# Six start addresses for the blocks of split weights, and three raw buffers for four, in a one-layer decoder kernel

## The chip, the cores and the metric

The kernel runs on one core of a Trainium2 chip. The metric is device time in microseconds (us), lower is better. A core has four engines that compute, each with its own in-order list of instructions: PE (matrix products, with a second record PEld for the loading of a product's stationary operand), DVE (elementwise arithmetic), ACT (elementwise functions and copies) and POOL. SP issues most of the transfers (DMA). All of them meet through semaphores only. SBUF is the memory on the core, 128 partitions wide; an address below is a byte offset within a partition.

## The reference

One decoder layer on 512 tokens of width 1024, with all weights in float32:

```python
h = h + 0.5 * swiglu(rms_norm(h, ffn1_norm), ffn1_w_gu, ffn1_w_down)      # width 2816
n = rms_norm(h, mix_norm)
p = n @ w_in + b_in                    # 6 x 1024 columns
a_val, a_gate, b_u, b_v, g_a, g_b = jnp.split(p, split_at, axis=-1)
y_a = conformer_conv_branch(a_val, a_gate, ...)   # GLU, causal depthwise conv of 31 taps, layer norm, swish, @ w_a_out
y_b = spatial_gating_branch(b_u, b_v, ...)        # gelu, layer norm, 128 x 128 mixing, @ w_b_out
h = h + (sigmoid(g_a) * y_a + sigmoid(g_b) * y_b) @ w_out
h = h + memory_cross_attention(rms_norm(h, xattn_norm), rms_norm(mem, mem_norm), w_q, w_kv, w_o)  # 4 heads, 256 memory tokens
h = h + 0.5 * swiglu(rms_norm(h, ffn2_norm), ffn2_w_gu, ffn2_w_down)
return rms_norm(h, final_norm)
```

## The kernel before

Activations lie channel-major: 8 tiles of 128 channels by 512 tokens, in `xhi`/`xlo` or in 50 slots of the pool `big`. Every float32 operand of a large product is split into two float32r parts, hi (a copy rounded to float32r) and lo (the rest), and `mm3` makes one product out of three matmuls: hi by hi (L106), hi weight by lo activation (L107), lo weight by hi activation (L108). In most stages the weight is the stationary operand, 128 by 128, and the activation moves with 512 columns. In `linear_rows` (L174 to L176) it is the other way round and the weight moves. The keys (`key`, tiles `pk`, 64 products) and the last output tile (`dl`, 44 products) have 256 columns.

Weights come in blocks of up to 128 by 1024 (512 KB). A block goes through three steps. `wfetch` takes a tile `raw` and issues its transfer on SP (L90). `wsplit` copies it on ACT to `hi` (L98, the CAST rows) and subtracts on DVE to get `lo` (L99). PE then reads `hi` and `lo`, 24 matmuls for a full block. There are four raw buffers, three for hi and three for lo, so a transfer waits until the DVE split of an earlier block has freed a raw buffer, and a CAST waits until PE is done with an earlier block. The memory tokens (`mem`, two blocks of 512 KB) come through the same raw buffers and are read straight from there by ACT and DVE (L185, L186, L190, L193). A raw buffer is freed by its last reader.

The order on each engine is set by a scheduler that estimates times from the program; code order is its input. A name such as `d3w8h` is the hi part of the block of `w_dn` for output tile 3 that begins at k = 8; `d3w` in a transfer's row is its raw buffer. The stages in order of time: `g`/`u` (first up projection), `d` (down projection, with the two `mem` blocks), `pk` (keys), `av`/`ag` (conv inputs), `r` (token-major rows), `gb`, `yb`, `ga`, `pv`, `ya`, `o`, attention (`pq`, `sc`, `po`, `wo`), `g`/`u` and `d` again. The depthwise convolution runs on DVE beside the matmuls (L346): tap `back` adds into a tile from element `back` on, so its output and one input begin 4 x `back` bytes into a slot and have 512 - `back` elements.

Of the kernel before, what the change touches and what calls it, by code (L numbers as in the profile page):

```python
# [10 lines left out]
F32 = mybir.dt.float32  # L11
F32R = mybir.dt.float32r
# [4 lines left out]
P = 128  # L17
# [26 lines left out]
NV = _o  # L44
VW = 416


@with_exitstack
def conformer_layer(ctx: ExitStack, tc: tile.TileContext, xT, memT, vecs, rows, w_gu1, w_dn1, w_in_f, w_in_t,
# [5 lines left out]
    wpool = ctx.enter_context(tc.tile_pool(name="wpool", bufs=1))  # L55
# [7 lines left out]
    h = const.tile([P, DT, T], F32, name="h")  # L63
# [19 lines left out]

    def wfetch(srcs, name):

        raw = wpool.tile([P, 1024], F32, tag="raw", name=name, bufs=4)
        n = 0
        for src in srcs:
            m = src.shape[1] * src.shape[2]
            nc.sync.dma_start(out=raw[:, n:n + m], in_=src.rearrange("p k c -> p (k c)"))  # L90
            n += m
        return raw[:, :n]

    def wsplit(raw, c, name):
        n = raw.shape[1]
        hi = wpool.tile([P, 1024], F32R, tag="whi", name=name + "h", bufs=3)[:, :n]
        lo = wpool.tile([P, 1024], F32R, tag="wlo", name=name + "l", bufs=3)[:, :n]
        S.copy(out=hi, in_=raw)  # L98
        V.tensor_tensor(out=lo, in0=raw, in1=hi.bitcast(F32), op=ALU.subtract)  # L99
        return hi.rearrange("p (k c) -> p k c", c=c), lo.rearrange("p (k c) -> p k c", c=c)  # L100

    def wload(src, name):
        return wsplit(wfetch([src], name), src.shape[2], name)
# [49 lines left out]
    def linear_pair(wsrcs, ahi, alo, name):  # L153

        accs = [new_ps(f"{name}{i}") for i in range(2)]
        for k0 in range(0, DT, DT // 2):
            ks = slice(k0, k0 + DT // 2)
            whi, wlo = wsplit(wfetch([w[:, ks, :] for w in wsrcs], f"{name}w{k0}"), P, f"{name}w{k0}")
            for k in range(k0, k0 + DT // 2):
                for i in range(2):  # L160
                    c = i * DT // 2 + k - k0
                    mm3(accs[i], whi[:, c, :], wlo[:, c, :], ahi[k], alo[k], k == 0, k == DT - 1)
        return accs
# [73 lines left out]
    def pair(name):  # L237
        return slot(name + "h", F32R), slot(name + "l", F32R)
# [29 lines left out]
    for k in range(DT):  # L268
        nc.sync.dma_start(out=h[:, k, :], in_=xT[:, k, :])
        if k == 0:  # L270
            nc.sync.dma_start(out=vec[:, :NV], in_=vecs)
        if k % 2 == 0:
            j, k0 = k // 2 % 2, k // HF * HF
            raws.append(wfetch([w_gu1[j][:, k0:k0 + HF, :], w_gu1[FT + j][:, k0:k0 + HF, :]], f"first{k}"))
    firsts = [(new_ps(f"fg{j}"), new_ps(f"fu{j}")) for j in range(2)]
    ws = []
    for k in range(DT):
        split_x(k, "ffn1_norm")
        if k % HF < 2:
            ws.append(wsplit(raws[len(ws)], P, f"first{k}"))  # L280
        if k % HF == 0:
            continue
        for kk in (k - 1, k) if k % HF == 1 else (k,):
            for j in range(2):
                whi, wlo = ws[kk // HF * 2 + j]
                for i in range(2):
                    c = i * HF + kk % HF
                    mm3(firsts[j][i], whi[:, c, :], wlo[:, c, :], xh[kk], xl[kk], kk == 0, kk == DT - 1)
# [227 lines left out]
    for i in range(DT):  # L516
# [6 lines left out]
        hi, lo = pair(f"aa{i}")  # L523
# [7 lines left out]
    for m in range(DT):  # L531
# [4 lines left out]
        hi, lo = pair(f"mg{m}")  # L536
# [13 lines left out]
    oh, ol = [], []  # L550
# [3 lines left out]
    for i in range(DT // 2):  # L554
        hi, lo = pair(f"k{i}")
# [111 lines left out]
    for i in range(2):  # L667
        ts = slice(i * T // 2, (i + 1) * T // 2)
        pd = new_ps(f"dl{i}")[:, :T // 2]
        for k in range(FT):  # L670
            whi, wlo = ws[k // 8]
# [71 lines left out]
```

## Time and profile before

| what | us |
|---|---|
| median of 2 runs | 1323.42 (1323.26 to 1323.59) |
| the profiled execution, whole | 1324.05 |
| its span, first to last instruction | 1322.3 |
| around the span | 1.75 |
| PE busy | 1299.4 (98%) |

The profiled execution is 0.63 us over the median, so a difference worked out on its rows is put on the median unchanged. Rows of PE overlap, since a matmul is pipelined: the time that one costs is the distance between two starts, and its own length says little. The rows of PEld lie under those of PE.

### The profile page before, as it was taken

Reading aid. Unit: us, or ns where it says so; the run is one execution under the profiler, and the core shown is the slowest. Engines: PE = TensorE matmul, PEld = TensorE weight load, DVE = VectorE, ACT = ScalarE, POOL = GpSimd, SP = SyncE. Lnnn points to the kernel's source line nnn. Section 1 sums busy time; section 2 is a strip of 40 time slices with the busy share of each in tenths; the row PEclk is TensorE's granted clock in tenths of the full one; section 3 lists DMA queues with packets and bytes.
Section 4 is the critical chain, followed back from the end, with each engine's and each line's share of the span. In section 5 each row is a group of like instructions: output and inputs, shape, how many; then the busy total and the mean of one; then the engine's idle time right before and its main releaser. Section 6 shows DMA issues by size and latency. Waiting matters only on the chain.

```text
span 1322.3 us, 14923 instructions
## 1 busy us (share of the span) xinstructions
PE 1299.4 (98%) x5968; PEld 1079.5 (82%) x5968; DVE 776.7 (59%) x1078; ACT 456.3 (35%) x618; POOL 19.4 (1%) x31
## 2 busy tenths in 40 slices
PE   7999999999999999999999999999999999999996
PEld 6888888888898888888788788887888888888886
DVE  5544444434367999999996776554644444442323
ACT  5323333223233223343224744333433332322221
POOL 0000000000020000100000000000000000000000
PEclk9999999999999999999999999999999999999998
DMA  6333323333353333332233333102332232333221
GB/s 212 108 98 98 96 96 96 88 101 114 112 183 114 102 96 96 104 98 78 93 98 113 110 112 110 66 20 72 127 101 96 96 96 96 96 88 104 88 72 64
DMA packets 40661, 132.47 MB, mean 100 GB/s; under 512 B 4433, under 2 KB 7249, under 8 KB 40593
## 3 DMA queue, kind: packets, MB, share of 16 engines
q1 hardware_dynamic: 39872, 129.17, 31.1%
q0 software_dynamic: 720, 2.36, 0.6%
q8 instruction: 46, 0.75, 0.2%
q14 instruction: 23, 0.18, 0.0%
HBM read 129.42 MB, written 2.10 MB: 99 GB/s over the span
## 4 chain that ended last, share of the span: by engine, by line
PE 97%; DVE 1%; ACT 1%; DMA 0%; issue 0%; SPq 0%; DVEq 0%; POOLq 0%; ACTq 0%
PE g L106 6%; PE u L107 6%; PE g L107 6%; PE u L106 6%; PE u L108 6%; PE g L108 6%; PE d L106 6%; PE d L108 6%; PE d L107 6%; PE r L175 2%; PE r L176 2%; PE r L174 2%; PE ya L106 1%; PE ya L107 1%; PE gb L108 1%; PE ga L106 1%
## 5 line engine op out<-in xcount | busy, mean ns | idle before, releaser
L346 DVE SCALAR_TENSOR_TENSOR cv<-ap,vec,cv 128x494 f32<-128x494 f32 (+24 forms) x240 | 163.4, 731 | 0.4
L246 DVE TENSOR_TENSOR u<-u,n4rb 128x512 f32<-128x512 f32 x22 | 15.2, 691 | 66.8 <-PE u L108 66.8
L246 DVE TENSOR_TENSOR u<-u,n1rb 128x512 f32<-128x512 f32 x20 | 13.8, 691 | 62.6 <-PE u L108 62.6
L242 DVE TENSOR_TENSOR g<-g,n4rb 128x512 f32<-128x512 f32 x22 | 15.2, 691 | 48.4 <-PE g L108 44.3
L242 DVE TENSOR_TENSOR g<-g,n1rb 128x512 f32<-128x512 f32 x20 | 13.8, 691 | 40.1 <-PE g L108 40.1
L248 DVE TENSOR_TENSOR f<-s,u 128x512 f32<-128x512 f32 x44 | 30.4, 692 | 5.4 <-ACT s L244 1.1
L244 ACT ACTIVATE s<-g 128x512 f32<-128x512 f32 x44 | 27.9, 633 | 0.1
L263 DVE SCALAR_TENSOR_TENSOR h<-d,h 128x512 f32<-128x512 f32 x15 | 10.4, 692 | 29.5 <-PE d L108 29.5
L194 DVE TENSOR_TENSOR acc<-acc,sq 128x512 f32<-128x512 f32 x34 | 23.3, 685 | 0.1
L193 ACT ACTIVATE sq<-h 128x512 f32<-128x512 f32 x34 | 21.2, 623 | 1.3 <-DVE h L263 0.2
L186 DVE SCALAR_TENSOR_TENSOR xlo<-h,vec,xhi 128x512 fp32r<-128x512 f32 x24 | 17.8, 747 | 5.0 <-ACT xhi L185 5.0
L185 ACT ACTIVATE xhi<-h,vec 128x512 fp32r<-128x512 f32 x24 | 17.2, 717 | 1.6 <-DVE h L628 1.1
L545 DVE TENSOR_TENSOR h<-o,h 128x512 f32<-128x512 f32 x8 | 5.5, 692 | 12.5 <-PE o L108 12.5
L534 DVE TENSOR_TENSOR ga<-ya,sga 128x512 f32<-128x512 f32 x8 | 5.5, 689 | 12.3 <-PE ya L108 12.3
L389 DVE TENSOR_TENSOR uv<-r,br 128x512 f32<-128x512 f32 x16 | 10.5, 687 | 0.1
L106 PE MATMUL fg<-xhi,first0h 128*128 128x512 f32 x4 | 2.2, 550 | 8.2 <-ACT first0h L98 8.2
L589 ACT ACTIVATE pr<-sc,mx 128x256 f32<-128x256 f32 x16 | 7.4, 470 | 6.4 <-DVE mx L586 6.4
L390 ACT ACTIVATE uv<-uv 128x512 f32<-128x512 f32 x16 | 9.0, 620 | 1.2 <-DVE uv L389 1.2
L569 DVE TENSOR_TENSOR qt<-pq,n3rb 128x512 f32<-128x512 f32 x8 | 5.3, 686 | 6.9 <-ACT n3rb L220 4.1
L628 DVE TENSOR_TENSOR h<-wo,h 128x512 f32<-128x512 f32 x8 | 5.4, 688 | 6.3 <-PE wo L108 6.3
L106 PEld LDWEIGHTS fg<-xhi,first0h 128*128 128x128 f32 x4 | 1.0, 251 | 8.4 <-ACT first0h L98 8.2
L585 DVE TENSOR_REDUCE mx<-sc 128x2 f32<-128x512 f32 x8 | 5.5, 692 | 3.7 <-PE sc L108 3.3
(4300 smaller groups left out, 4251.1 us busy)
## 6 DMA issues: line engine op xcount, KB each, us to landing
h<-xT SPq DMA_DIRECT2D x8, 256.0 KB, 5.8
first<-w_gu SPq DMA_DIRECT2D x8, 256.0 KB, 5.9
d0w<-w_dn SPq DMA_DIRECT2D x4, 512.0 KB, 3.5
d1w<-w_dn SPq DMA_DIRECT2D x4, 512.0 KB, 3.7
d2w<-w_dn SPq DMA_DIRECT2D x4, 512.0 KB, 3.4
d3w<-w_dn SPq DMA_DIRECT2D x4, 512.0 KB, 3.4
d4w<-w_dn SPq DMA_DIRECT2D x4, 512.0 KB, 3.6
d5w<-w_dn SPq DMA_DIRECT2D x4, 512.0 KB, 3.5
```

What stands on the lines that cost most here:

```text
L106: PE.matmul(out, whi, ahi, start=start, stop=False)
L107: PE.matmul(out, whi, alo, start=False, stop=False)
L108: PE.matmul(out, wlo, ahi, start=False, stop=stop)
L174: PE.matmul(accs[t], a_h, whi[:, k - k0, :], start=k == 0, stop=False)
L175: PE.matmul(accs[t], a_h, wlo[:, k - k0, :], start=False, stop=False)
L176: PE.matmul(accs[t], a_l, whi[:, k - k0, :], start=False, stop=k == nk - 1)
L194: V.tensor_tensor(out=acc, in0=acc, in1=sq, op=ALU.add)
L242: V.tensor_tensor(out=g1, in0=pg, in1=rb, op=ALU.mult)
L244: S.activation(s1, g1, AF.Silu)
L246: V.tensor_tensor(out=u1, in0=pu, in1=rb, op=ALU.mult)
L248: V.tensor_tensor(out=f, in0=s1, in1=u1, op=ALU.mult)
L346: V.scalar_tensor_tensor(out=o, in0=aps[i][:, :T - back], scalar=w, in1=o, op0=ALU.mult, op1=ALU.add)
```

## The change

The tiles of hi and lo grow by 64 elements, and the block lies in them at an offset that goes round with every third block: hi at element 0, 16 or 32 (byte 0, 64, 128), lo at element 4, 2 or 48 (byte 16, 8, 192). In the kernel before, all hi, lo and raw tiles begin at multiples of 256 bytes, as all slots of `big` do, and a product's 128 by 128 weights follow each other at 512 bytes. After the change hi lies at multiples of 64 bytes, one lo in three too, one lo in three 16 bytes and one in three 8 bytes past such a multiple. The raw pool has three tiles in place of four. The six larger tiles take 1.5 KB more and the missing raw tile 4 KB less, so `big` and the pools behind it move down by 2,560 bytes and stay at multiples of 256. The offsets go round in step with the three buffers, so each buffer keeps one place.

```diff
+SHIFTS = ((0, 4), (16, 2), (32, 48))
...
     def wfetch(srcs, name):
-        raw = wpool.tile([P, 1024], F32, tag="raw", name=name, bufs=4)
+        raw = wpool.tile([P, 1024], F32, tag="raw", name=name, bufs=3)
...
+    shift = [0]
+
     def wsplit(raw, c, name):
         n = raw.shape[1]
-        hi = wpool.tile([P, 1024], F32R, tag="whi", name=name + "h", bufs=3)[:, :n]
-        lo = wpool.tile([P, 1024], F32R, tag="wlo", name=name + "l", bufs=3)[:, :n]
+        oh, ol = SHIFTS[shift[0] % 3]
+        shift[0] += 1
+        hi = wpool.tile([P, 1024 + 64], F32R, tag="whi", name=name + "h", bufs=3)[:, oh:oh + n]
+        lo = wpool.tile([P, 1024 + 64], F32R, tag="wlo", name=name + "l", bufs=3)[:, ol:ol + n]
         S.copy(out=hi, in_=raw)
         V.tensor_tensor(out=lo, in0=raw, in1=hi.bitcast(F32), op=ALU.subtract)
```

The instructions are the same ones. On PE, POOL and SP they also keep their order, apart from what they wait for. On ACT and DVE the order differs at two places. The lines of the changed kernel have numbers higher by 6 (L98 there is L104). The first place is in the first down projection, where ACT reads the first memory block (m0h, m2h, macc) between the CASTs of weight blocks. Before:

```order
L98 CAST d1w16h<-d1w_1935 128x768
L190 ACTIVATE acc_1786<-h 128x512
L185 ACTIVATE m0h<-mem_2052,vec 128x256
L190 ACTIVATE macc<-mem_2052 128x256
L185 ACTIVATE m0h<-mem_2052,vec 128x256
L185 ACTIVATE m2h<-mem_2052,vec 128x256 x2
L98 CAST d2w0h<-d2w_1964 128x1024
L98 CAST d2w8h<-d2w_1994 128x1024
L98 CAST d2w16h<-d2w_2024 128x768
```

and after:

```order
L104 CAST d1w16h<-d1w_1935 128x768
L196 ACTIVATE acc_1786<-h 128x512
L104 CAST d2w0h<-d2w_1964 128x1024
L191 ACTIVATE m0h<-mem_2052,vec 128x256
L196 ACTIVATE macc<-mem_2052 128x256
L191 ACTIVATE m0h<-mem_2052,vec 128x256
L104 CAST d2w8h<-d2w_1994 128x1024
L191 ACTIVATE m2h<-mem_2052,vec 128x256 x2
L104 CAST d2w16h<-d2w_2024 128x768
```

The CASTs of d2w0 and d2w8 have moved ahead of readers of the memory block, and the splits of these two blocks on DVE likewise. The second place is on ACT at the end of the attention's output projection, where xhi and sq prepare the next norm. Before:

```order
L98 CAST wo5w0h<-wo5w_7029 128x1024
L185 ACTIVATE xhi<-h,vec 128x512
L190 ACTIVATE acc_6150<-h 128x512
L185 ACTIVATE xhi<-h,vec 128x512
L193 ACTIVATE sq<-h 128x512
L98 CAST wo6w0h<-wo6w_7066 128x1024
L185 ACTIVATE xhi<-h,vec 128x512
L193 ACTIVATE sq<-h 128x512
```

and after:

```order
L104 CAST wo5w0h<-wo5w_7029 128x1024
L191 ACTIVATE xhi<-h,vec 128x512
L196 ACTIVATE acc_6150<-h 128x512
L191 ACTIVATE xhi<-h,vec 128x512
L199 ACTIVATE sq<-h 128x512
L191 ACTIVATE xhi<-h,vec 128x512
L199 ACTIVATE sq<-h 128x512
L104 CAST wo6w0h<-wo6w_7066 128x1024
```

The CAST of wo6w0 stands one pair of xhi and sq later, and its split on DVE one xlo later.

## Rows read from the trace of the kernel before

**Rows 1.** Page, part 1: busy us, share of the span, instructions.

```profile
PE 1299.4 (98%) x5968; PEld 1079.5 (82%) x5968; DVE 776.7 (59%) x1078; ACT 456.3 (35%) x618; POOL 19.4 (1%) x31
```

**Rows 2.** Page, part 4: the chain that ended last.

```profile
PE 97%; DVE 1%; ACT 1%; DMA 0%; issue 0%; SPq 0%; DVEq 0%; POOLq 0%; ACTq 0%
```

**Rows 3.** Timeline, down projection: start us, length us, what; 42 matmuls apart.

```profile
299.87 0.39 PE L108 MATMUL d<-f4h,d3w0l 128*128 128x512 f32 x1
...
309.39 0.39 PE L108 MATMUL d<-f18h,d3w16l 128*128 128x512 f32 x1
```

**Rows 4.** Windows: busy us of the engines, granted clock (1.00), DMA share, GB/s.

```profile
290.00:300.00 10.00, 10.00 (x46) 8.29 (x45) 4.19 (x6) 3.45 (x6) 0.00 (x0) 1.00 0.40 113
```

**Rows 5.** Timeline of PE, keys with 256 columns, 16 matmuls apart.

```profile
381.90 0.28 PE L106 MATMUL pk<-m0h,pk3w0h 128*128 128x256 f32 x1
...
383.82 0.28 PE L107 MATMUL pk<-m4l,pk3w0h 128*128 128x256 f32 x1
```

**Rows 6.** Groups of PEld, down projection: busy us, mean ns of one.

```profile
L108 PEld LDWEIGHTS d<-f5h,d0w0l 128*128 128x128 f32 x1 | 0.2, 188 | 0.0
```

**Rows 7.** Groups by form of DVE, convolution taps, 380 to 640 us.

```profile
L346 DVE SCALAR_TENSOR_TENSOR cv<-ap,vec,cv 128x510 f32<-128x510 f32 x8 | 6.0, 748 | 0.0
L346 DVE SCALAR_TENSOR_TENSOR cv<-ap,vec,cv 128x508 f32<-128x508 f32 x7 | 5.2, 743 | 0.0
L346 DVE SCALAR_TENSOR_TENSOR cv<-ap,vec,cv 128x496 f32<-128x496 f32 x6 | 4.4, 727 | 0.0
```

**Rows 8.** Transfers: count, KB each, median us to landing; av2w is the longest.

```profile
d5w<-w_dn SPq DMA_DIRECT2D x4, 512.0 KB, 3.5
...
av2w<-w_in_f SPq DMA_DIRECT2D x1, 512.0 KB, 7.5
```

**Rows 9.** Timelines of SP and DVE at the start.

```profile
10.39 1.01 SPq L90 DMA_DIRECT2D first<-w_gu  x2
...
8.17 1.23 DVE L99 TENSOR_TENSOR first0l<-first,first0h 128x1024 fp32r<-128x1024 f32 x1 [2.39 <-ACT first0h L98]
```

**Rows 10.** Timelines of SP, ACT and DVE, down projection with its memory blocks.

```profile
268.65 0.33 SPq L90 DMA_DIRECT2D mem<-memT  x1
...
272.25 0.51 ACT L185 ACTIVATE m0h<-mem,vec 128x256 fp32r<-128x256 f32 x1 [3.92 <-DMA mem<-memT]
277.68 1.05 ACT L98 CAST d2w8h<-d2w 128x1024 fp32r<-128x1024 f32 x1 [2.47 <-issue]
...
281.94 0.69 DVE L263 SCALAR_TENSOR_TENSOR h<-d,h 128x512 f32<-128x512 f32 x1 [1.95 <-PE d L108]
308.68 1.23 DVE L99 TENSOR_TENSOR d4w8l<-d4w,d4w8h 128x1024 fp32r<-128x1024 f32 x1 [3.42 <-ACT d4w8h L98]
317.12 1.05 ACT L98 CAST d5w0h<-d5w 128x1024 fp32r<-128x1024 f32 x1 [3.90 <-PE d L107]
357.26 0.90 ACT L185 ACTIVATE m6h<-mem,vec 128x256 fp32r<-128x256 f32 x2
```

**Rows 11.** Transfers of yaw; timelines of DVE, ACT and PE before the product with w_a.

```profile
DMA to landing us min/median/max: 2.9/3.8/4.0
...
730.64 1.22 DVE L99 TENSOR_TENSOR pv1w4l<-pv1w,pv1w4h 128x1024 fp32r<-128x1024 f32 x1
735.39 1.06 ACT L98 CAST yaw4h<-yaw 128x1024 fp32r<-128x1024 f32 x1 [0.34 <-PE pv L176]
737.43 1.37 ACT L460 ACTIVATE vt<-pv,nmr 128x512 f32<-128x512 f32 x2 [0.46 <-PE pv L176]
738.70 0.61 ACT L181 CAST aa0h<-lny 128x512 fp32r<-128x512 f32 x1
739.36 0.73 PE L106 MATMUL ya<-aa0h,yaw0h 128*128 128x512 f32 x2 [1.28 <-ACT aa0h L181]
```

**Rows 12.** Timelines of ACT and PE, attention's output projection.

```profile
926.51 1.05 ACT L98 CAST wo6w0h<-wo6w 128x1024 fp32r<-128x1024 f32 x1
935.63 0.39 PE L106 MATMUL wo<-oo0h,wo6w0h 128*128 128x512 f32 x1
```

## Prediction

> **What bounds the kernel now.** I read the page's busy times first: PE is busy 98% of the span, every other engine at most 59%, but for the weight loads that run under PE's own matmuls [rows 1]. A busy PE is not yet PE at its peak, so the chain of work that ended last comes next: 97% of it is PE, and the transfers, SP and the other engines together hold 2% [rows 2]. So the time is a number of matmuls times the distance between two starts, plus a few places where PE waits. That distance is read off a timeline. In the down projection 42 matmuls of 512 columns take 309.39 - 299.87 = 9.52 us, 226.7 ns each [rows 3], at a granted clock of 1.00, the 2.4 GHz level [rows 4]. 512 columns at 2.4 GHz are 213.3 ns, so 13.4 ns in each matmul are not columns. A matmul of 256 columns takes 1.92 us / 16 = 120 ns [rows 5], 13.3 ns over its 106.7. The excess is thus the same for a long and a short matmul.
>
> Two things can move the time: the 226.7 ns, if PE reads the shifted blocks differently, and the places where PE waits for a block, since blocks now have three raw buffers.
>
> **The change part by part.**
>
> *Where PE reads hi and lo.* No instruction is added, so the price is a change of the distance times a count. The 5,968 matmuls [rows 1] are at most 5,968 / 3 = 1,989 that read a lo, and two lo in three leave the 64-byte multiples: 1,326 at most. All hi and the remaining lo stay at multiples of 64 bytes. No operand of PE before lies 8 or 16 bytes off such a multiple at full width, so the trace doesn't show this read, and I bound it. What is near: DVE reads and writes shifted runs all through the convolution, and a run of 510 elements that begins at byte 8 takes 748 ns, one of 508 at byte 16 743, one of 496 at byte 64 727 [rows 7]. That is 21 ns for 14 elements, which falls smoothly with the count and has no step between 8, 16 and 64 bytes. On PE a load takes 188 ns of the 226.7 ns of its matmul [rows 6], so 38.7 ns may be added before one is late. I take 0, by the rows of DVE and that cover. If the cover goes, the price is in the second rival below; the other end is the whole 13.4 ns given back, the first rival.
>
> *What DVE and ACT write.* The split on DVE now writes lo at byte 8, 16 or 192, and ACT writes hi at 0, 64 or 128. By the same rows of DVE this costs nothing. A change of 10 ns in one of some 245 splits would be 2.5 us of DVE time in all, on an engine that is 59% busy [rows 1, 7]. I put it at 0.
>
> *Three raw buffers, at the start.* Each transfer of a block waits until the DVE split of the block three places earlier (before: four) is through, and SP issues in order, so everything behind it waits too. The first wait that is new is that of the fourth block: it needs the split of first0, which ends at 8.17 + 1.23 = 9.40 us. Its transfer is issued at 10.39 anyway [rows 9], so neither it nor the last slice of h behind it on SP is later. Cost 0.
>
> *Three raw buffers, in the stages.* A full block is 24 x 0.2267 = 5.44 us of PE, so a transfer that waits for one block more comes about 5.4 us later. The least cover is in the down projection, because a memory block keeps its raw buffer long: the second has landed by about 304 us and its last part is first read at 357.26 [rows 10]. Two buffers are then left for the weights. Take d5w0: its transfer must now wait for the split of d4w8, which ends at 308.68 + 1.23 = 309.91; with 3.5 us to landing [rows 8] it is there at 313.4, and its CAST starts at 317.12, released by PE [rows 10]. 3.7 us are left. Cost 0.
>
> *The memory blocks themselves and the moved CASTs.* The first memory block loses its cover altogether: m0h starts the moment it lands, 268.65 + 3.6 = 272.25. Now the transfer waits for the split of d2w0. The CAST of d2w0, which the new order puts first, can start one block before that of d2w8, at 277.68 - 5.44 = 272.24; its split on DVE ends some 2.3 us later (1.05 + 1.23), at 274.5, and the block lands at 278.1. ACT waits there, and behind m0h, macc and m0h (at most 0.51 us each) stands the CAST of d2w8: it starts at about 279.6 in place of 277.68, and lo is done at 281.9. PE ends the tile before at 281.94 and needs d2w8 a block later, at 287.4 [rows 10]. The cover is 5.5 us, so cost 0. The second memory block makes d4w8 late by about the same 2 us; that turns the 3.7 us above into 1.7, still positive.
>
> *The product with w_a.* Here PE does wait: 1.28 us until aa0h [rows 11]. The second block of yaw could be issued when pv1w2 was split; now it waits for pv1w4, split at 730.64 + 1.22 = 731.86. Two issues of some 0.4 us apart and at most 4.0 us to landing give 736.2, where its CAST started at 735.39. So the CAST is about 0.9 us late. ACT is in order, and behind the CAST are queued vt and then aa0h, which ends PE's wait. vt itself waited 0.46 us for PE, so ACT had that much room [rows 11]. What is left is 0.9 - 0.46 = 0.4 us, and from then on PE has no other work to fill it: **+0.4 us**. It is the one place where I find the depth of the buffers on the path.
>
> *The attention's output.* The CAST of wo6w0 is moved behind one more xhi and sq and its transfer waits one block longer. It stood at 926.51, and PE first reads it at 935.63 [rows 12]. After 2.3 us of split 6.8 us of cover remain, for a move of 1 to 2 us. Cost 0.
>
> The sum is +0.4 us: 1324.05 becomes 1324.45 for the profiled execution, and on the median 1323.42 + 0.4 = **1323.8 us**.
>
> **The rivals.**
>
> *The excess is a conflict of places, and the shift removes it.* If loads and moving reads meet in the same part of SBUF because all begin at multiples of 256 bytes, six places would take them apart. At most all 5,968 matmuls lose 13.4 ns: 80 us, 1243 us. For it speaks only that the excess is there and that all places before are round. Against it: weights at six buffers and in eight steps of 512 bytes, beside moving operands at other places, all give the one distance, as 42 in a row show [rows 3]; and the excess is 13.3 ns for half the columns too [rows 5], where a conflict in streaming would halve.
>
> On this the Trainium skill, "TensorE: Matmul & The Clock Gate", section "Wait — 56ns, not 53.3ns?", has 215.7 ns from start to start for 512 columns when warm; this trace is 11 ns above it. As an estimate from that page, 5,968 x 11 ns = 66 us would be to be had, 1258 us. The same page, section "Step-by-step: what each phase is for", says that the load and the moving operand have read ports of their own, so a load takes nothing from the running matmul; by that rule the places can't matter and this rival falls. The trace agrees as far as it goes, since loads lie under matmuls that keep one distance.
>
> *A shifted lo costs its load a second pass* (the other side). If a start off the line makes PE read a column's words twice, the load is doubled at two lo in three. It decides when a load takes over 226.7 ns. The load's share of PE's time is between 120 ns, since PE loads once every 120 ns in the narrow products [rows 5], and 188 ns [rows 6]. Doubled, the first is 240: 13.3 ns over, on the wide ones; the 64 + 44 narrow products hold 72 shifted lo, at 120 ns more each. (1,326 - 72) x 13.3 + 72 x 120 = 25 us, 1349 us. Doubled, the second is 376: 1,326 x 149.3 = 198 us, 1521 us. Against it: DVE's shifted runs cost nothing [rows 7]; for it, that PE's loads are another reader and this read has no row.
>
> *Two raw buffers are too few beside a memory block.* A buffer is busy for the time to landing plus 2.3 us of split, and two of them feed PE while (landing + 2.3) / 2 is under 5.44, which is up to a landing of 8.6 us. The median is 3.5 and the longest for a weight block in one view 7.5 [rows 8]. Were it 10 us for the 20 or so blocks there, each would cost 0.7 us: 14 us, 1338 us. That takes landings nobody sees in this trace.
>
> **How the numbers follow.** The forecast, no change but for a wait of 0.4 us, gets 0.81; the conflict that is removed 0.05; the second pass 0.10, half of it under 2%; the starved buffers 0.04, of which a quarter over 2%. A measurement of this kernel tells about 2% from no change, 26 us. So faster by over 2% is 0.05, slower 0.05 + 0.01 = 0.06, and within 0.89. For the range I take the forecast with about 5 us below, for a partial gain on PE and the chip's own spread, and 10 us above, for a load that is late at few places or waits that I priced at 0: 1319 to 1334. What is left out is most of the rivals, 0.17 or so.
>
> **What would show it.** In the changed kernel's timeline of the down projection 42 matmuls should still take 9.52 us, and matmuls on L114, which read lo, should lie as close as those on L112, in blocks at byte 8 and 16 as at 192. A larger distance on L114 alone would be the second pass; a smaller one on all three lines the conflict. Loads should stay near 188 ns. SP's own waits should grow by about a block, the CASTs in the down projection should still be released by PE and not by transfers, apart from the memory blocks, and the CAST of yaw4 should come near 736.2 with PE's wait for aa0h near 1.7 us. I am wrong if any CAST but those of the memory blocks and yaw4 ends its wait on a transfer and PE waits behind it, or if the distance moves by over 5 ns.

## The result, and the profile after

The changed kernel takes 1343.88 us (median of 2 runs, 1343.66 to 1344.09) against 1323.42: a ratio of 1.0155, with a 95% interval of 1.0111 to 1.0198. The forecast was 1323.8, in 1319 to 1334. It is 20.5 us slower than before, and 9.9 us above the upper end of that range.

Page of the changed kernel, its first line, the busy times and the chain of work that ended last:

```profile
span 1342.4 us, 14921 instructions
PE 1320.0 (98%) x5968; PEld 1079.6 (80%) x5968; DVE 777.1 (58%) x1078; ACT 456.0 (34%) x618; POOL 19.4 (1%) x31
PE 97%; ACT 1%; DVE 1%; DMA 0%; issue 0%; SPq 0%; DVEq 0%; POOLq 0%; ACTq 0%
```

Beside [rows 1, 2] one number has moved: PE is busy 1320.0 us in place of 1299.4, 20.6 us more, with the same 5,968 matmuls. Loads (PEld), DVE and ACT are where they were, and the chain is 97% PE as before. The span less PE's busy time is 22.4 us, before 22.9. So PE didn't wait longer; its matmuls lie further apart.

What PE waited for, in the changed kernel: the wait, then us in total, times, longest us:

```profile
PE fg L112 <- ACT first0h L104: 7.7, 1, 7.7
...
PE po L112 <- ACT ph L187: 2.3, 4, 0.6
...
PE ya L112 <- ACT aa0h L187: 1.3, 1, 1.3
```

The wait before the product with w_a, which the forecast put at 1.7 us, is 1.3 as in [rows 11]. No transfer stands in this list.

Windows of the changed kernel, the same ten microseconds as [rows 4]; the granted clock is the third number from the end, 1.00:

```profile
290.00:300.00 10.00, 10.00 (x46) 8.18 (x45) 2.45 (x2) 2.10 (x2) 0.00 (x0) 1.00 0.28 87
```

The clock is the 2.4 GHz level in both, so it is no part of this.

Timeline of PE in the changed kernel, first the up projection, then the down projection; each row is the first of a block's 24 matmuls of 512 columns, so a difference of two starts, divided by 24, is the distance:

```profile
72.87 0.39 PE L112 MATMUL u<-xhi,u5w0h 128*128 128x512 f32 x1
...
78.47 0.40 PE L112 MATMUL g<-xhi,g6w0h 128*128 128x512 f32 x1
...
84.04 0.40 PE L112 MATMUL u<-xhi,u6w0h 128*128 128x512 f32 x1
...
89.59 0.39 PE L112 MATMUL g<-xhi,g7w0h 128*128 128x512 f32 x1
...
95.17 0.39 PE L112 MATMUL u<-xhi,u7w0h 128*128 128x512 f32 x1
...
100.61 0.40 PE L112 MATMUL g<-xhi,g8w0h 128*128 128x512 f32 x1
...
301.55 0.39 PE L112 MATMUL d<-f0h,d3w0h 128*128 128x512 f32 x1
...
307.12 0.39 PE L112 MATMUL d<-f8h,d3w8h 128*128 128x512 f32 x1
...
312.56 0.40 PE L112 MATMUL d<-f16h,d3w16h 128*128 128x512 f32 x1
```

u5 has hi at byte 128 and lo at 192, g6 0 and 16, u6 64 and 8, then again g7 128 and 192, u7 0 and 16. Their blocks take 5.60, 5.57, 5.55, 5.58 and 5.44 us: 233.3, 232.1, 231.3, 232.5 and 226.7 ns. In the down projection d3w0 (128 and 192) takes 5.57 and d3w8 (0 and 16) 5.44 us. So the distance that was 226.7 ns in [rows 3] has risen by up to 6.6 ns, it differs from block to block, and the place whose hi and lo both lie at multiples of 64 bytes is the worst of the three. It also differs between blocks with the same places: u7 and d3w8 keep 226.7 ns although their lo begins at byte 16, and g6, at the same places, doesn't. Worked out from all starts of PE in the two traces, the 5,370 matmuls of 512 columns stand 232.9 ns apart on the mean, before 228.9 (waits included in both): 5,370 x 3.97 = 21.3 us. The 474 of 256 columns went from 123.1 to 121.7 ns, 0.7 us back. Together that is 20.6 us, what PE's busy time grew by.

The excess is on all three lines, not on the reads of lo alone: L112 (hi against hi) rises by 4.6 ns, L113 (hi against lo) by 3.1, L114 (lo against hi) by 4.0. And the load itself is no longer than in [rows 6]: the mean of all 5,968 is 187.8 ns, before 187.9. Loads of a lo at byte 16 and of a hi at byte 0 in the changed kernel (ns min/median/max, first and last start):

```profile
L114 PEld LDWEIGHTS d<-f9h,d3w8l x1: 187/187/187, 308.0 to 308.0; 128*128 128x128 f32 x1
```

```profile
L112 PEld LDWEIGHTS d<-f9h,d3w8h x1: 188/188/188, 307.6 to 307.6; 128*128 128x128 f32 x1
```

### The profile page after: what moved, and what is told of

Its sections match the earlier page's. It is cut to its first block, busy times and chain, and to the rows that moved or that the text cites. A ratio compares the mean times of both kernels' runs of the same rounds, so it can differ in the third digit from the quotient of the medians.

```text
span 1342.4 us, 14921 instructions
## 1 busy us (share of the span) xinstructions
PE 1320.0 (98%) x5968; PEld 1079.6 (80%) x5968; DVE 777.1 (58%) x1078; ACT 456.0 (34%) x618; POOL 19.4 (1%) x31
## 4 chain that ended last, share of the span: by engine, by line
PE 97%; ACT 1%; DVE 1%; DMA 0%; issue 0%; SPq 0%; DVEq 0%; POOLq 0%; ACTq 0%
PE g L112 6%; PE g L114 6%; PE u L112 6%; PE g L113 6%; PE u L114 6%; PE u L113 6%; PE d L112 6%; PE d L114 6%; PE d L113 6%; PE r L182 2%; PE r L181 2%; PE r L180 2%; PE ya L112 1%; PE ya L113 1%; PE ag L112 1%; PE ga L112 1%
## 5 line engine op out<-in xcount | busy, mean ns | idle before, releaser
L551 DVE TENSOR_TENSOR h<-o,h 128x512 f32<-128x512 f32 x8 | 5.5, 692 | 13.4 <-PE o L114 13.3
L112 PE MATMUL fg<-xhi,first0h 128*128 128x512 f32 x4 | 2.2, 554 | 7.7 <-ACT first0h L104 7.7
```

The costliest lines, as they stand in the source:

```text
L112: PE.matmul(out, whi, ahi, start=start, stop=False)
```

## The experiments

All but one (pad64) keep the three raw buffers. Most place the blocks through one table of pairs (hi, lo), which counts elements of 4 bytes; the text gives bytes. Where no number of runs is given, a kernel ran once.

**Which half of the change is it?** Three raw buffers alone:

```
-SHIFTS = ((0, 4), (16, 2), (32, 48))
+SHIFTS = ((0, 0),)
-        hi = wpool.tile([P, 1024 + 64], ...)
+        hi = wpool.tile([P, 1024], ...)          # lo the same
```

> Three raw buffers, hi and lo where they were. If the loss is in where PE reads (the place theory), this kernel has the time of before, 1323 to 1325 us, and a matmul of 512 columns starts every 226.7 ns. If the third raw buffer matters (the depth theory), it shows here alone: more than 1326 us, with PE waiting behind CASTs.

Measured: 1323.83 us (10 runs) beside 1323.40, ratio 1.0003, interval 0.9993 to 1.0013. No cost of the depth can be told from nothing, so the loss is that of the places. Timelines of SP, ACT, DVE and PE of this kernel, at the first memory block and before the product with w_a:

```profile
273.35 0.33 SPq L92 DMA_DIRECT2D mem<-memT  x1
...
271.01 1.05 ACT L104 CAST d2w0h<-d2w 128x1024 fp32r<-128x1024 f32 x1 [3.90 <-PE d L113]
277.09 0.51 ACT L191 ACTIVATE m0h<-mem,vec 128x256 fp32r<-128x256 f32 x1 [5.02 <-DMA mem<-memT]
278.21 1.03 ACT L104 CAST d2w8h<-d2w 128x1024 fp32r<-128x1024 f32 x1
...
315.89 1.05 ACT L104 CAST d5w0h<-d5w 128x1024 fp32r<-128x1024 f32 x1 [3.90 <-PE d L113]
...
729.44 1.22 DVE L105 TENSOR_TENSOR pv1w4l<-pv1w,pv1w4h 128x1024 fp32r<-128x1024 f32 x1
...
734.19 1.06 ACT L104 CAST yaw4h<-yaw 128x1024 fp32r<-128x1024 f32 x1 [0.34 <-PE pv L182]
...
738.15 0.73 PE L112 MATMUL ya<-aa0h,yaw0h 128*128 128x512 f32 x2 [1.28 <-ACT aa0h L187]
```

At the memory block it went as forecast, some 1.2 us earlier on the clock: the block is issued after the split of d2w0, m0h waits 5.02 us for it, the CAST of d2w8 stands right behind, and no wait of PE follows. d5w0's CAST is still released by PE. Before the product with w_a it did not: the CAST of yaw4 stands 4.75 us behind the split of pv1w4, in [rows 11] 735.39 - 730.64 = 4.75 as well, and is released by PE, not by its transfer.

**Which shift costs?** hi and lo together at 64 bytes; lo alone; and all 16 pairs of 0, 64, 128 and 192 bytes by turns, three blocks each:

```
+SHIFTS = ((16, 16),)                             # both64
+SHIFTS = ((0, 16),)                              # lo64
+SHIFTS = ((0, 0), (0, 16), ... (48, 48))         # scan64, 16 pairs
+        oh, ol = SHIFTS[shift[0] // 3 % len(SHIFTS)]
```

> Three raw buffers, tiles of 1152 elements, hi and lo both at byte 64 in every block. If the place of a load against the moving operand counts: the distance leaves 226.7 ns, 229 to 233, so 1337 to 1356 us. If only the place of hi against lo counts, or only a start off the 64-byte multiples: 226.7 ns and 1323 to 1325 us.

> Three raw buffers, tiles of 1152 elements, hi at byte 0, lo at byte 64 in every block. If the place against the moving operand counts, or that of hi against lo: 229 to 233 ns, 1337 to 1356 us. If a start off the 64-byte multiples counts: 226.7 ns, 1323 to 1325 us.

> Three raw buffers, tiles of 1152 elements, all 16 pairs of hi and lo at byte 0, 64, 128 and 192, each for three blocks in a row. Place against the moving operand: only the pair 0, 0 keeps 226.7 ns, the others lie between 224 and 234. Place of hi against lo: the four equal pairs keep 226.7, the rest doesn't. Start off 64 bytes: all pairs keep 226.7.

Measured: 1352.78, 1344.40 and 1346.26 us, beside 1323.40. Timelines of PE in the down projection, first of both64, then of lo64:

```profile
303.55 0.39 PE L112 MATMUL d<-f0h,d3w0h 128*128 128x512 f32 x1
...
309.15 0.39 PE L112 MATMUL d<-f8h,d3w8h 128*128 128x512 f32 x1
```

```profile
300.26 0.39 PE L112 MATMUL d<-f0h,d3w0h 128*128 128x512 f32 x1
...
305.81 0.39 PE L112 MATMUL d<-f8h,d3w8h 128*128 128x512 f32 x1
```

5.60 / 24 = 233.3 ns with both shifted alike, 5.55 / 24 = 231.3 with lo alone. So a multiple of 64 bytes is no safe place, no doubled load is needed for the loss, and hi and lo need not differ from each other: both64 is the slowest of the three. In scan64 only the pair (0, 0) keeps the distance. Its timeline of PE, where d2w0 is the last block at (0, 0) and d2w8 the first at (0, 64):

```profile
286.51 0.39 PE L112 MATMUL d<-f0h,d2w0h 128*128 128x512 f32 x1
...
291.95 0.39 PE L112 MATMUL d<-f8h,d2w8h 128*128 128x512 f32 x1
...
297.49 0.39 PE L112 MATMUL d<-f16h,d2w16h 128*128 128x512 f32 x1
```

5.44 us is 226.7 ns, 5.54 us 230.8. The other fourteen, like (0, 64), are slower; as means over their blocks all fifteen lie between 229 and 234 ns.

**Is it the place in SBUF, or the place against the other operand, and how fine?** Four kernels: all tiles of the kernel before moved by 64 bytes, with four raw buffers; the weights at 256 bytes; pairs of 4 to 224 bytes; and twenty pairs drawn at random between 0 and 252 bytes, to see whether any is better than before.

```
+    pad = const.tile([P, 16], F32, name="pad")   # pad64: ahead of all tiles of the kernel before
+    nc.gpsimd.memset(pad, 0.0)
+SHIFTS = ((64, 64),)                             # w256
+SHIFTS = ((1, 1), (2, 2), (4, 4), ... (8, 0))    # scan_fine, 16 pairs
+SHIFTS = ((32, 45), (3, 59), ... (49, 38))       # scan_mixed, 20 pairs
```

> The kernel before with 64 bytes put ahead of all its tiles, so that weights and moving operands all lie 64 bytes past a multiple of 256 and stand to each other as before. If the place of the load against the moving operand counts (relative theory): 226.7 ns, 1323 to 1325 us. If an operand must start at a multiple of 256 bytes (absolute theory): 229 to 233 ns, 1337 to 1356 us.

> Three raw buffers, tiles of 1152 elements, hi and lo at byte 256 in every block: still multiples of 256, but 256 bytes against the moving operand modulo 512. If 256 bytes is the period of the pattern: 226.7 ns, 1323 to 1325 us. If it is 512: another distance, 229 to 233 ns.

> Three raw buffers, tiles of 1152 elements, each pair of places for three blocks: hi and lo both at 4, 8, 16, 32, 48, 96, 160 or 224 bytes, then one of them at 0 and the other at 4, 8, 16 or 32. If what counts is the line of 64 bytes in which a run starts, the small steps below 64 keep 226.7 where they start in the same line; if every byte of distance counts, they spread from 224 to 235 like those of 64. Relative and absolute theory both leave this open.

> Three raw buffers, tiles of 1152 elements, 20 pairs of places drawn at random between 0 and 252 bytes, each for three blocks. If the places of before are the best there are, no pair has a mean under 226.5 ns; if they are one of many, some pairs lie between 216 and 226.

Measured: 1324.07, 1324.26, 1353.64 and 1353.49 us, beside 1323.15 for the kernel before. With every operand moved alike nothing to speak of is lost (0.9 us, beside 20 to 30 for the kernels with shifted weights), so by this run it isn't where a tile lies but how operands lie to each other. Weights moved by 256 bytes are as good as unmoved ones, and by 64, 128 or 192 they aren't (scan64), so the place counts modulo 256 bytes. Timelines of PE, one block each, first of pad64, then of w256, 5.44 us in both:

```profile
66.25 0.39 PE L108 MATMUL g<-xhi,g5w0h 128*128 128x512 f32 x1
...
71.69 0.39 PE L108 MATMUL u<-xhi,u5w0h 128*128 128x512 f32 x1
```

```profile
66.89 0.39 PE L112 MATMUL g<-xhi,g5w0h 128*128 128x512 f32 x1
...
72.33 0.39 PE L112 MATMUL u<-xhi,u5w0h 128*128 128x512 f32 x1
```

One thing here rests on the code and not on a trace, since no trace shows an address. That a block begins so many bytes into its tile is certain. That pad64 moved every tile by 64 bytes, and that weights and activations agreed in the kernel before, supposes that tiles are packed as their sizes say. (`vec`, the first tile, has 416 x 4 = 1,664 bytes, 6.5 times 256. Packed behind it, the others would all begin 128 bytes past a multiple of 256, not at one as said further up, and would still agree with one another.) And of all the runs only pad64, run once, was made to tell the relative theory from the absolute one. If it is read so, both64 names one relation that counts: there, where weights are the stationary operand, all loads lie alike and all moving operands lie alike, and only loads and moving operands differ, by 64 bytes.

And of scan_fine, d2w0 at (4, 4) bytes, then d3w0 at (8, 8):

```profile
288.76 0.39 PE L112 MATMUL d<-f0h,d2w0h 128*128 128x512 f32 x1
...
294.33 0.39 PE L112 MATMUL d<-f8h,d2w8h 128*128 128x512 f32 x1
...
304.02 0.39 PE L112 MATMUL d<-f0h,d3w0h 128*128 128x512 f32 x1
...
309.56 0.39 PE L112 MATMUL d<-f8h,d3w8h 128*128 128x512 f32 x1
```

One element off costs nearly as much as sixteen: 5.57 us, 232.1 ns. None of the sixteen pairs of this scan is free: their means are 230.7 to 234.2 ns. In scan_mixed no pair but (0, 0) comes to 226.7 ns; the means of the others are 231 to 235.

**Need the weights be moved at all?** If it is the relation of operands, moving activations alone must cost the same. xlo moved by 64 bytes, weights at 0; then xlo and the weights' lo moved by 64 together; and, as the other side, six places as in the change but all at multiples of 256 bytes:

```
+    xlo = const.tile([P, DT * T + 64], F32R, name="xlo")[:, 16:16 + DT * T].rearrange(...)
+SHIFTS = ((0, 0),)                               # xlo64
+SHIFTS = ((0, 16),)                              # xlo_lo64
+SHIFTS = ((0, 64), (64, 128), (128, 0))          # six256, xlo as before
```

> Three raw buffers, hi and lo of the weights at multiples of 256 bytes as before; of the moving operands xlo alone lies 64 bytes on, in the stages that read xhi and xlo. If the distance depends on how a load stands to the moving operand: it rises in those stages to 229 to 234 ns and stays at 226.7 in the down projections, 1331 to 1345 us. If shifted weights are slow as such: 226.7 ns everywhere, 1323 to 1325 us.

> Three raw buffers; xlo and the lo of the weights both lie 64 bytes on. The load of a lo runs under the matmul before it, which moves xlo, and the matmul that uses it moves xhi. If a load counts against the operand that moves while it runs: 226.7 ns in the up projections (every load stands to the stream above it as before) and about 231 ns in the down projections, where the slots are not shifted, 1330 to 1334 us. If it counts against the operand of its own matmul, or hi against lo: about 231 ns in both, 1340 to 1346 us.

> The changed kernel with other places: hi at byte 0, 256 or 512, lo at 256, 512 or 0, tiles of 1152 elements, three raw buffers. If only the place modulo 256 bytes against the moving operand counts: 226.7 ns and 1323 to 1325 us, no difference from before. If six places cost as such: 1337 to 1356 us.

Measured: 1340.20 and 1345.09 us, and 1323.20 (10 runs) for six256, beside 1323.49; for six256 that is a ratio of 0.9998, with an interval of 0.9989 to 1.0008. Timeline of PE in xlo64, a block that reads xhi and xlo, then one of the down projection, which doesn't:

```profile
67.10 0.39 PE L112 MATMUL g<-xhi,g5w0h 128*128 128x512 f32 x1
...
72.66 0.40 PE L112 MATMUL u<-xhi,u5w0h 128*128 128x512 f32 x1
...
301.30 0.39 PE L112 MATMUL d<-f0h,d3w0h 128*128 128x512 f32 x1
...
306.74 0.39 PE L112 MATMUL d<-f8h,d3w8h 128*128 128x512 f32 x1
```

5.56 us (231.7 ns) against 5.44 (226.7): the loss is in the stages that read xlo, and the down projection has none of it. ACT and DVE write hi and lo where they did before, and write xlo no more after 20 us until the next norm, so the loss is one of PE's own reads and not of a meeting with those writes. In the up projections all three lines carry it (from the start of a matmul on L112 to the next start 231.3 ns on the mean, on L113 232.1, on L114 232.6). The last goes from a lo against xhi to a hi against xhi, neither of which reads xlo: so what PE read shortly before counts too, not a matmul's own pair alone. In xlo_lo64 the two moved operands agree with each other and not with the unmoved ones; its block takes 5.55 us (231.3 ns), so agreement of a load with the stream that it runs under isn't enough:

```profile
67.65 0.40 PE L112 MATMUL g<-xhi,g5w0h 128*128 128x512 f32 x1
...
73.20 0.40 PE L112 MATMUL u<-xhi,u5w0h 128*128 128x512 f32 x1
```

six256 moves weights between six places as the change does and keeps 5.44 us:

```profile
65.81 0.39 PE L112 MATMUL g<-xhi,g5w0h 128*128 128x512 f32 x1
...
71.25 0.39 PE L112 MATMUL u<-xhi,u5w0h 128*128 128x512 f32 x1
```

**Is a matmul's agreement with its own operands enough?** The k-th slice of weights and the k-th slice of xhi and xlo are all put at 64 x k bytes, so that within a matmul all agree, and one k differs from the next:

```
+    xhi = const.tile([P, DT, T + 16], F32R, name="xhi")[:, :, :T]    # xlo the same
+        e = n // c * (c + 16)
+        hi = wpool.tile([P, 1152], ...)[:, :e].rearrange("p (k c) -> p k c", c=c + 16)[:, :, :c]   # lo the same
```

> Three raw buffers. In the stages that read xhi and xlo, each channel tile k of xhi and xlo and each 128 columns of hi and lo for that k lie 64 x k bytes past a multiple of 256: a matmul's own load and stream agree modulo 256 always, and with those of the next k never. If a load counts against the stream of its own matmul: 226.7 ns in the up projections; in the down projections the slots don't step and the distance rises, about 1332 us. If all loads and streams that follow each other must agree: 229 to 234 ns in both, 1340 to 1356 us. If only loads and streams at the change of k matter: one matmul in three is later, about 228 to 229 ns in the up projections.

Measured: 1346.43 us beside 1323.60. A block in the up projection, timeline of PE:

```profile
66.23 0.39 PE L112 MATMUL g<-xhi,g5w0h 128*128 128x512 f32 x1
...
71.80 0.39 PE L112 MATMUL u<-xhi,u5w0h 128*128 128x512 f32 x1
```

5.57 us, 232.1 ns. Agreement within each matmul isn't enough either: it is lost from one k to the next, and the distance with it.

**Can the narrow matmuls gain?** In the changed kernel the 256-column products came closer together. This kernel moves the weights of the keys and of the last tile alone, by 64 bytes:

```
+        oh, ol = (16, 16) if name[:2] in ("pk", "dl") else (0, 0)
```

> Three raw buffers, tiles of 1152 elements; only the blocks of the keys and of the last output tile, whose matmuls have 256 columns, lie at byte 64, all others at byte 0. In the runs with shifted blocks the narrow matmuls came 114 to 118 ns apart against 120 before. If that holds by itself: 324 narrow matmuls save some 4 to 5 ns each, 1.3 to 1.6 us, so about 1322 us, a ratio near 0.999 that the rounds may just tell from 1. If the narrow ones gained only from what stood before them: 1323 to 1324 us.

Measured: 1322.79 us (11 runs) beside 1323.40, ratio 0.9995, interval 0.9986 to 1.0004: not told apart from no change. The timeline of PE does show it, 16 matmuls of the keys:

```profile
381.16 0.28 PE L112 MATMUL pk<-m0h,pk3w0h 128*128 128x256 f32 x1
...
383.05 0.28 PE L113 MATMUL pk<-m4l,pk3w0h 128*128 128x256 f32 x1
```

1.89 / 16 = 118 ns, in [rows 5] 120. Over all 436 narrow matmuls that follow one another without a wait, the mean is 117.1 against 119.2 ns: 0.9 us, a size that the interval neither shows nor excludes. No version run here clearly beats the kernel before.

## Why the prediction was wrong

**Where PE reads hi and lo** is the step that failed. It took 0 for the distance, between -13.4 ns and a doubled load of lo, and counted only lo at 8 and 16 bytes as moved. Measured: +4.0 ns on the mean of 5,370 wide matmuls, 21.3 us, in all three kinds of product and most in the place where hi and lo are at multiples of 64. Two pieces of its reasoning don't carry. The shifted runs of DVE [rows 7] say nothing of PE, and DVE did stay at its price here (777.1 us against 776.7). And "all places give the one distance" rested on places that all agreed modulo 256 bytes: steps of 512 bytes, tiles of 4096 [rows 3]. six256 and w256 show that such places indeed give one distance; no shifted pair in scan64 and scan_fine does. The cover of 38.7 ns between load and matmul [rows 6] was no cover either: the load stays at 188 ns on the mean and the distance grows all the same.

**The first rival** had the right variable, how operands lie to each other, and the wrong sign. The kernel before, with all of them in agreement, is not the worst case but the best of those tried: of some fifty pairs of places in three scans none with a shift is better. That two reads meet in one part of SBUF, as this rival has it, no run shows. Beside it stood a page of the Trainium skill, "TensorE: Matmul & The Clock Gate", section "Step-by-step: what each phase is for", by which the load and the moving operand have read ports of their own. The prediction drew from it that places couldn't matter, and that doesn't follow: in xlo64, with the same loads and the same work, the distance is 226.7 or 231.7 ns by the place of one operand alone. Whether the ports are separate no run here shows.

**The second rival**, a second pass of the load, falls: loads take as long as before, L112 and L113 rise too, and lo64, with lo at a multiple of 64, costs as much as the change. That it came near the loss (25 us forecast, 20.5 measured) is chance.

**Three raw buffers**, at the start, in the stages, at the memory blocks and before the attention's output, were put at 0, and three_raw agrees within what it can tell: 0.4 us over the kernel before, a ratio of 1.0003 in 0.9993 to 1.0013. **The product with w_a** was put at +0.4 us with PE's wait at 1.7; it is 1.28 in three_raw and 1.3 after. That term was mis-sized too, by 0.4 us: I took the longest landing, 4.0 us, and in three_raw those of yaw took less. Transfers of yaw in that kernel:

```profile
DMA to landing us min/median/max: 2.6/3.1/3.5
```

With 3.5 us for 4.0 the forecast's 736.2 becomes 735.7, with the median of 3.1 it is 735.3, against a CAST at 735.39: on time, or late by less than the 0.46 us of room it had found in vt. **What DVE and ACT write** was right at 0.

**The chances and the range.** The slower side held 0.06 by the bound of 2%; the loss is 1.55%, within that bound, but it lies 10 us above the range, whose upper side allowed for late loads at a few places and not for a few nanoseconds at every matmul. One nanosecond on 5,370 matmuls is 5.4 us; a range for an edit that moves every weight block of a PE-bound kernel had to be made in that unit. The signs of being wrong had the same flaw. 42 matmuls of the down projection take 9.61 us in the changed kernel (304.80 to 314.41), not 9.52, and the growth on all three lines is one that neither rival had; yet the mean moved by 4.0 ns, less than the 5 ns that were to count as wrong, and 5 ns would have been 27 us.

## What to carry to other kernels

In a kernel of float32r products that is bound by PE, keep the start addresses of all operands that PE reads one after the other, weights and activations, equal modulo 256 bytes: pad tiles by multiples of 256 and look at the addresses again after any change of a tile's size. Here a start only 4 bytes off made the distance 2 to 3% longer, and no shift that was tried made that of 512 columns shorter. Evidence that "place doesn't matter" covers only the residues that were seen, so before taking 0 for a new one, ask in what way all the old ones were alike.

## What the runs showed of the hardware

The distance between two matmuls of 512 columns depends on how their operands lie to each other modulo 256 bytes: 226.7 ns when all agree, and 229 to 235 as means of the shifted pairs in the three scans, at the same granted clock and with loads of 188 ns on the mean. That it is the relation and not the place itself is shown by pad64 alone. Agreement kept the 226.7 ns wherever it was tried; it isn't always needed, as u7 and d3w8 of the changed kernel show. The DVE, in contrast, reads and writes shifted runs at about the price of unshifted ones: it is busy 777.1 us in the changed kernel and 776.7 before.

What stays open: by what mechanism places act, since moving a stream (xlo64), a load (lo64) or one k against the next (step64) all cost about 5 ns; why one pair of places has two distances (0 and 16 bytes in the changed kernel: 226.7 in u and d, 232.1 in g, the same in every round through the up projection). The pairs of places before and behind it are the same in both cases, so a block's own places and its neighbours' don't settle it; the block before took 233.3 ns (u5, before g6) or 232.5 (g7, before u7), and what is carried over isn't known. Also open are why 256 columns go the other way and come closer, 120 to 118 ns; and where the 13.4 ns over 512 columns come from that remain when all agree. Places were tried only in these forms, so a better order of places than full agreement isn't excluded, only not found.
